# One step of a two-branch diffusion backbone in fp32 on one core: the residual kept in DRAM between the two halves of the output projection, and lanes and loaded weights in the lasting pool

## The chip, the cores and the metric

The kernel runs on 1 core of one Trainium2 chip. The metric is the device time of one execution in microseconds (us); the time of a kernel is the median of several runs. One execution is also recorded by the hardware profiler, and all rows below are from that one.

## The reference, cut to what matters

640 tokens (512 latent, 128 context) of width 2048 go through one layer. Everything is fp32. The modulation vectors come from a product of the conditioning vectors with a weight of 2048 x 12288.

```python
mod_ctx = silu(c_ctx) @ w_ada + b_ada        # the same for the latent tokens with c
shift1, scale1, gate1, shift2, scale2, gate2 = split(mod, 6)
h = rms_norm(x, g_norm1) * (1 + scale1) + shift1
proj = h @ w_in                              # query, compressed kv, rotary key, and three conv streams
attn = attention(...)                        # 8 heads, 1024 columns
conv = short_conv(...)                       # 1024 columns
mixed = concat([rms_norm(attn, g_attn_out), rms_norm(conv, g_conv_out)]) @ w_out
x = x + gate1 * mixed
h2 = rms_norm(x, g_norm2) * (1 + scale2) + shift2
gate, up = split(h2 @ w_gate_up, 2)          # 2 x 5632 columns
x = x + gate2 * ((silu(gate) * up) @ w_down)
y = rms_norm(x, g_final)
```

## The kernel before

All matrices lie transposed, features on the 128 partitions and the 640 tokens in two halves of 320, so a tensor of width 2048 is 16 tiles `R` of 128x640. Each fp32 product is made of three: both sides are split into a high and a low part (`split`: ScalarE casts the high part, L139, VectorE subtracts it, L140; `split_mul`, L144/L145, does so with a factor), and TensorE multiplies high by high, high by low and low by high (`mm3`, L162). A weight block of 512 KB is loaded by the SP queue into a `wr` tile and split by `wsplit` into `wh` and `wl`.

The stages follow each other, and one scheduler with a timeline model sets the order of the instructions on each engine ahead of time; the tile pools add the waits for free buffers.

- The modulation's first third (`ada1`) and eight early columns of the input projection.
- 31 more input projections (`proj`), 24 of them for the convolution branch, then attention over 8 heads.
- The output projection in two parts of 16 half projections each (one 512 KB weight and 48 matmuls of width 320 for each). Part 1 takes the convolution heads `nv`; it makes the gated residual `x1[m]` with `add_gated` (one VectorE multiplication, L606, and two VectorE additions with a scalar, L608). Beside it `na`, the attention heads with their gain, are split (L139, L145). Part 2 takes `na`, adds to `x1[m]` in place, sums its squares (`add_sq`: ScalarE square, L223, GpSimd addition, L224, VectorE for the last two), multiplies by the second scale into `u` (L670), stores `x1[m]` to DRAM (L673), and for each pair of m makes the seven-product operands `hs` (`splits`: sums on L636 to L639, casts and splits by L139 and L140).
- `r2 = rstd(ssq)`, the second rms factor: a matmul with ones (L205), logarithm and exponential on ScalarE (L207, L211), four VectorE steps (L208, L212 to L214).
- The first half of the feed-forward: 44 mids, and in each four units of 42 matmuls (`seven`, L715: seven products p1 to p3, each of two k-steps and three part products). `weights` loads 512 KB, sums three blocks (L697 to L699) and splits the loaded part (128x768) and the summed part (128x1024) on L139 and L140. VectorE then combines the seven PSUM banks (L735 to L741), GpSimd multiplies gate and up by `r2` (L742, L743), and ScalarE and VectorE make silu times up (L745, L746). `keep` and `sums` write the split results to DRAM (`parts`).
- The second half (`w_down`, also by `seven`), which loads `parts` by GpSimd's queue (L774), then a short tail.

The rest of the modulation (`ada2`) is work in the background: 8 blocks of 16 steps; a step loads 512 KB into `aw` and makes two VectorE operations of 128x1024 on `acc` (L260, L262), and a block ends with matmuls, a copy and additions (L269 to L279). `background(2)` is called with each weight split and gives out `RATES` steps for each of the two; `rest_of_background` gives out all that are left.

Memory: the pool `sb` lasts the whole program and holds 57 tiles `R`. The lanes `T1`, `T2` and `acc`, `aw`, `wr`, `wh`, `wl` are in a pool `first` that is closed at the end of the output projection; a pool `second` with `T1`, `T2`, `wr`, `ws`, `wh`, `wl` takes its place. In part 2 the 57 tiles hold `na` (16), `x1` (16), `ra`, `ssq`, and 7 for each pair of `hs`, so that from the fifth pair on `hs` waits for tiles of `na`, which the last half projection of part 2 reads.

## Time and profile before

| what | us |
|---|---|
| median of 3 runs | 2748.19 |
| lowest and highest | 2748.03, 2751.26 |
| the profiled execution | 2750.71 |
| its span | 2748.9 |
| TensorE busy in it | 2671.1 (97%) |
| VectorE busy in it | 2214.3 (81%) |

PE is TensorE's matmul stream, DVE is VectorE, ACT ScalarE, POOL GpSimd, SP the queue that loads weights. A row of the timeline gives the start, the duration, the instruction, and in brackets how long its engine stood idle before it and what released it. Rows of equal instructions are merged (x4) and their duration is that of all of them; since matmuls are pipelined, the distance of two starts tells more than a duration.

### The profile page before, as it was taken

To read this page: it belongs to the slowest core of one execution; us is meant where nothing else is said; L and a number is where in the kernel's file an instruction comes from. 1 tells how busy PE (TensorE), PEld (TensorE's weight loads), DVE (VectorE), ACT (ScalarE), POOL (GpSimd) and SP (SyncE) were. 2 spreads that over 40 slices of the span, in tenths; PEclk is the share of its full clock that TensorE was granted. 3 is DMA by queue.
4 is the path that set the end of the run, shared out by engine and by line. 5 is a ranking of instruction groups with operands and counts; after the bars stand their busy time and mean duration, and the time that the engine had idled before them with its cause. 6 is when DMAs were issued, how large, how long until landed. Compare 5 with 4: busy or idle time off the path is not lost.

```text
span 2748.9 us, 46698 instructions
## 1 busy us (share of the span) xinstructions
PE 2671.1 (97%) x18840; PEld 2625.9 (96%) x18840; DVE 2214.3 (81%) x3257; ACT 1024.5 (37%) x1550; POOL 402.5 (15%) x395
## 2 busy tenths in 40 slices
...
GB/s 306 288 191 187 185 192 175 189 182 62 16 151 178 187 161 83 120 123 147 118 131 139 118 152 118 123 147 119 131 139 128 272 230 156 290 161 178 214 186 143
DMA packets 156776, 447.85 MB, mean 163 GB/s; under 512 B 17104, under 2 KB 27792, under 8 KB 156560
## 3 DMA queue, kind: packets, MB, share of 16 engines
...
HBM read 366.66 MB, written 78.15 MB: 162 GB/s over the span
## 4 chain that ended last, share of the span: by engine, by line
PE 92%; DVE 4%; ACT 2%; issue 1%; DMA 1%; SPq 0%; ACTq 0%; DVEq 0%
PE bank L715 58%; PE psA L162 27%; PE bank L847 2%; PE psA L533 1%; PE psB L240 1%; DVE wl L140 1%; PE psB L562 1%; DVE acc L262 1%; DVE r L140 0%; PE psB L557 0%; ACT wh L139 0%; PE psB L269 0%; DMA t<-x 0%; DVE r L608 0%; ACT r L139 0%
## 5 line engine op out<-in xcount | busy, mean ns | idle before, releaser
L715 PE MATMUL bank<-r,wh 128*128 128x322 f32 (+1 forms) x7168 | 1594.5, 311 | 9.3 <-ACT wh L139 5.8
L715 PEld LDWEIGHTS bank<-r,wh 128*128 128x128 f32 x7168 | 1209.7, 189 | 10.6 <-ACT wh L139 6.8
L715 PE MATMUL bank<-r,wl 128*128 128x322 f32 (+1 forms) x3584 | 1112.8, 311 | 2.3 <-DVE wl L140 2.3
L139 ACT CAST wh<-wr 128x768 fp32r<-128x768 f32 (+1 forms) x370 | 333.0, 901 | 1121.6 <-issue 504.9
L162 PE MATMUL psA<-r,wh 128*128 128x322 f32 (+1 forms) x3584 | 693.5, 315 | 25.8 <-ACT r L139 11.0
L715 PEld LDWEIGHTS bank<-r,wl 128*128 128x128 f32 x3584 | 678.5, 189 | 2.7 <-DVE wl L140 2.7
L140 DVE TENSOR_TENSOR wl<-wr,wh 128x768 fp32r<-128x768 f32 (+1 forms) x370 | 422.9, 1143 | 246.1 <-ACT wh L139 245.8
L162 PEld LDWEIGHTS psA<-r,wh 128*128 128x128 f32 x3584 | 569.6, 190 | 41.5 <-ACT r L139 12.1
L162 PE MATMUL psA<-r,wl 128*128 128x322 f32 (+1 forms) x1792 | 415.9, 314 | 0.4 <-DVE wl L140 0.4
L140 DVE TENSOR_TENSOR wl<-ws,wh 128x1024 fp32r<-128x1024 f32 x256 | 366.0, 1430 | 31.2 <-ACT wh L139 31.1
L262 DVE SCALAR_TENSOR_TENSOR acc<-aw,sc,acc 128x1024 f32<-128x1024 f32 x240 | 302.6, 1299 | 7.9 <-DMA aw<-ada 7.8
L162 PEld LDWEIGHTS psA<-r,wl 128*128 128x128 f32 x1792 | 303.6, 190 | 3.4 <-issue 2.6
L139 ACT CAST wh<-ws 128x1024 fp32r<-128x1024 f32 x256 | 268.4, 1048 | 90.3 <-DVE ws L699 90.3
L743 POOL TENSOR_TENSOR t<-t,r 128x640 f32<-128x640 f32 x44 | 68.8, 1564 | 914.9 <-DVE t L740 914.9
L224 POOL TENSOR_TENSOR r<-r,t 128x640 f32<-128x640 f32 x42 | 79.0, 1880 | 811.7 <-ACT t L223 766.0
L697 DVE TENSOR_TENSOR ws<-wr 128x512 f32<-128x512 f32 x256 | 177.4, 693 | 5.5
L698 DVE TENSOR_TENSOR ws<-ws,wr 128x256 f32<-128x256 f32 x256 | 108.0, 422 | 5.6
L699 DVE TENSOR_TENSOR ws<-ws,wr 128x256 f32<-128x256 f32 x256 | 108.8, 425 | 4.4
L774 POOL DMA_DIRECT2D r<-parts x140 | 77.2, 564 | 159.5 <-PE bank L715 105.4
L355 DVE TENSOR_TENSOR r<-psA,r 128x644 f32<-128x644 f32 x64 | 52.4, 824 | 53.6 <-PE psA L162 53.6
L742 POOL TENSOR_TENSOR t<-t,r 128x640 f32<-128x640 f32 x44 | 93.6, 2127 | 0.8 <-DVE t L741 0.8
L745 ACT ACTIVATE t<-t 128x512 f32<-128x512 f32 x88 | 44.8, 557 | 111.8 <-POOL t L742 111.8
(180 smaller groups left out, 1907.3 us busy)
## 6 DMA issues: line engine op xcount, KB each, us to landing
...
aw<-ada SPq DMA_DIRECT2D x128, 512.0 KB, 4.3
parts<-t ACTq DMA_DIRECT2D x140, 320.0 KB, 4.2
r<-parts POOLq DMA_DIRECT2D x140, 320.0 KB, 6.7
...
```

The costliest lines, as they stand in the source:

```text
L139: A.copy(hi, src)
L140: return V.tensor_tensor(lo, src, hi.bitcast(F32), op=ALU.subtract)
L162: newest[T] = T.matmul(out[:, j, 0:n], w[p], x[q][:, j, 0:n], start=first and i == 0, stop=last and i == 2).ins
L224: e.tensor_tensor(acc, acc, qv, op=ALU.add)
L262: V.scalar_tensor_tensor(acc[v], w, sc[:, k, v:v + 1], acc[v], op0=ALU.mult, op1=ALU.add)
L697: V.tensor_tensor(q[:, :, 0:2], b[:, :, 1:4:2], b[:, :, 0:1].broadcast_to([P, 2, 2, P]), op=ALU.add)
L698: V.tensor_tensor(q[:, :, 2], q[:, :, 1], b[:, :, 1], op=ALU.add)
L699: V.tensor_tensor(q[:, :, 3], q[:, :, 2], b[:, :, 2], op=ALU.add)
L715: newest[T] = T.matmul(ps[name][:, 0:n], w[p][:, kp, i, :], xs[kp][x][q][:, 0:n], start=u + kp + t == 0, stop=u == len(units) - 1 and kp + ...
L742: G.tensor_tensor(row(g), row(g), r2, op=ALU.mult)
L743: G.tensor_tensor(row(up), row(up), r2, op=ALU.mult)
L774: nc.gpsimd.dma_start(t, two(parts[i][:, k], 320))
```

## The change

- In part 1, `add_gated` stores each `x1[m]` to DRAM from ScalarE's queue; in part 2 the SP queue loads it two half projections ahead into a fresh `R` tile and `add_gated` stores the sum again (before, it stayed in its tile and was stored once). So the 16 tiles of `x1` no longer stay.
- The last two `na` tiles lie in the buffers of `acc` and `aw` instead of `R`, and `u` of m = 10 to 13 lies in `R`.
- `T1`, `T2` and `wr` move from `first` and `second` to the lasting pool; `second` has one tile `hl` for high and low parts in the place of `wh` and `wl`.
- The rates of the modulation sums: 0.92 in the convolution projections (0.85), 1.1 in the query projections, 0 in attention, 0.83 in part 1 (0.85); what is left comes after m = 13 of part 1, and none in part 2 (0.6).
- `rstd` for the second factor is called between the second and the third unit of the first mid. Its matmuls go to two separate banks, and it writes into `ssq`.
- In the last two mids VectorE in place of GpSimd multiplies by the factor.

The diff:

```diff
--- before.py
+++ after.py
@@ -40,7 +40,9 @@
 
-FIRST = dict(T1=4, T2=3, acc=2, aw=2, wr=3, wh=3, wl=3)
-SECOND = dict(T1=4, T2=3, wr=3, ws=1, wh=3, wl=3)
+
+LASTS = dict(T1=4, T2=3, wr=3)
+FIRST = dict(acc=2, aw=2, wh=3, wl=3)
+SECOND = dict(ws=1, hl=3)
 NEARLY = 8
 GROUPS = [(0,), (1,)] + [(k, k + 1) for k in range(2, KT, 2)]
-RATES = (0.85, 0.0, 0.85, 0.6)
+RATES = (0.92, 1.1, 0.83)
 
@@ -50,2 +52,3 @@
             ("p4", 2, "t4", 322), ("p5", 4, "n1", 320), ("p3", 6, "b22", 320))
+LASTING = (10, 11, 12, 13)
 LAG = 1
@@ -86,6 +89,6 @@
     def T1(dtype=F32, shape=(P, 2, 320), name="t1"):
-        return bpool.tile(list(shape), dtype, name=name, tag="T1", bufs=bufs["T1"])
+        return pool.tile(list(shape), dtype, name=name, tag="T1", bufs=LASTS["T1"])
 
     def T2(dtype=F32, shape=(P, 2, 320), name="t2"):
-        return bpool.tile(list(shape), dtype, name=name, tag="T2", bufs=bufs["T2"])
+        return pool.tile(list(shape), dtype, name=name, tag="T2", bufs=LASTS["T2"])
 
@@ -95,3 +98,4 @@
     def tagged(tag, shape, n=None, dtype=F32):
-        return bpool.tile(list(shape), dtype, name=tag, tag=tag, bufs=n or bufs[tag])
+        p = pool if tag in LASTS else bpool
+        return p.tile(list(shape), dtype, name=tag, tag=tag, bufs=n or LASTS.get(tag) or bufs[tag])
 
@@ -197,3 +201,3 @@
 
-    def rstd(ssq, width, halves=(0, 1), out=None, wide=False):
+    def rstd(ssq, width, halves=(0, 1), out=None):
 
@@ -201,9 +205,7 @@
         v, t = T2(), T1()
-        pa = psA() if wide else None
-        ps = {j: pa[:, j, 0:320] if wide else psB()[:, 0:320] for j in halves}
-        for j in halves:
-            T.matmul(ps[j], ones, ssq[:, j, :], start=True, stop=True)
         for j in halves:
-            A.activation(t[:, j, :], ps[j], AF.Ln, bias=eps, scale=1.0 / width)
-            V.tensor_scalar(v[:, j, :], ps[j], 1.0 / width, EPS, op0=ALU.mult, op1=ALU.add)
+            ps = psB()[:, 0:320]
+            T.matmul(ps, ones, ssq[:, j, :], start=True, stop=True)
+            A.activation(t[:, j, :], ps, AF.Ln, bias=eps, scale=1.0 / width)
+            V.tensor_scalar(v[:, j, :], ps, 1.0 / width, EPS, op0=ALU.mult, op1=ALU.add)
         hs = slice(halves[0], halves[-1] + 1)
@@ -450,2 +452,3 @@
         add_sq(cssq, t, c == 0)
+    credit[1] = RATES[1]
     for h in range(1, NH):
@@ -573,4 +576,4 @@
 
-    def gain(t, g):
-        hl = R(F32R), R(F32R)
+    def gain(t, g, brief=False):
+        hl = [tagged(tag, (P, 2, 320), dtype=F32R) if brief else R(F32R) for tag in ("acc", "aw")]
         split_mul(*hl, t, g)
@@ -578,3 +581,3 @@
 
-    credit[1] = RATES[1]
+    credit[1] = 0.0
     kv = kv_pair(0)
@@ -603,3 +606,3 @@
 
-    def add_gated(ps, r, m):
+    def add_gated(x, ps, r, m):
         t = T1()
@@ -607,5 +610,6 @@
         for v, f in PARTS:
-            V.scalar_tensor_tensor(f(x1[m]), f(t), mod2[:, m, v:v + 1], f(x1[m]), op0=ALU.mult, op1=ALU.add)
+            V.scalar_tensor_tensor(f(x), f(t), mod2[:, m, v:v + 1], f(x), op0=ALU.mult, op1=ALU.add)
+        nc.scalar.dma_start(two(x1d[m], 320), x)
 
-    x1 = []
+    x1d = [dr(f"x1_{m}", (P, 640)) for m in range(KT)]
     credit[1] = RATES[2]
@@ -619,9 +623,11 @@
         for m in range(KT):
-            ps = proj(a["w_out"][m], nv, (0,))
-            x1.append(R())
-            nc.sync.dma_start(x1[m], a["x"][m])
-            add_gated(ps, rc, m)
+            x = R()
+            nc.sync.dma_start(x, a["x"][m])
+            add_gated(x, proj(a["w_out"][m], nv, (0,)), rc, m)
+            if m == 13:
+                rest_of_background()
+                credit[1] = 0.0
             if m >= 8:
                 with after(last_of(A), last_of(V)):
-                    na.append(gain(attn.pop(0), cst("gattn")[:, m - 8:m - 7]))
+                    na.append(gain(attn.pop(0), cst("gattn")[:, m - 8:m - 7], m > 13))
             if m == 12:
@@ -661,14 +667,17 @@
     hs, us = [], []
-    x1d = [dr(f"x1_{m}", (P, 640)) for m in range(KT)]
-    credit[1] = RATES[3]
+    x1 = {}
     for m in range(KT):
-        add_gated(proj(a["w_out"][m], na, (1,)), ra, m)
-        add_sq(ssq, x1[m], m == 0, G if m < KT - 2 else V)
+        for i in range(m, min(m + 2, KT)):
+            if i not in x1:
+                x1[i] = R()
+                nc.sync.dma_start(x1[i], two(x1d[i], 320))
+        x = x1[m]
+        add_gated(x, proj(a["w_out"][m], na, (1,)), ra, m)
+        add_sq(ssq, x, m == 0, G if m < KT - 2 else V)
 
-        u = (T1 if m % 2 else T2)(F32, (P, 2, 322))
+        u = (R if m in LASTING else T1 if m % 2 else T2)(F32, (P, 2, 322))
         for v, f in PARTS:
-            A.mul(f(u), f(x1[m]), mod2[:, 32 + m, v:v + 1])
+            A.mul(f(u), f(x), mod2[:, 32 + m, v:v + 1])
         G.tensor_copy(u[:, 0, 320:322], mod2[:, 16 + m, :])
         G.memset(u[:, 1, 320:322], 0.0)
-        nc.scalar.dma_start(two(x1d[m], 320), x1[m])
         us.append(u)
@@ -677,9 +686,7 @@
             us = []
-    del na, x1
+    del na, x1, x
 
 
-    r2 = rstd(ssq, D, wide=True)
     psums.close()
     psum = psums.enter_context(tc.tile_pool(name="ps8", bufs=1, space=bass.MemoryType.PSUM, reuse_waits="tile"))
-    rest_of_background()
     brief_pools.close()
@@ -694,3 +701,4 @@
         nc.sync.dma_start(b, src)
-        hi, lo = tagged("wh", (P, 2, 7, P), dtype=F32R), tagged("wl", (P, 2, 7, P), dtype=F32R)
+        hl = tagged("hl", (P, 2, 2, 7, P), dtype=F32R)
+        hi, lo = hl[:, 0], hl[:, 1]
         split(hi[:, :, 0:3], lo[:, :, 0:3], b[:, :, 1:4])
@@ -703,3 +711,3 @@
 
-    def seven(units):
+    def seven(units, between=None):
 
@@ -707,2 +715,5 @@
         for u, (src, xs) in enumerate(units):
+            if u == 2 and between:
+                with after(newest[T]):
+                    between()
             w = weights(src)
@@ -730,3 +741,5 @@
     for i in range(NMID):
-        ps = seven([(a["w_gu"][i, u], hs[2 * u:2 * u + 2]) for u in range(NU)])
+        ps = seven([(a["w_gu"][i, u], hs[2 * u:2 * u + 2]) for u in range(NU)],
+                   None if i else lambda: rstd(ssq, D, out=ssq))
+        r2 = ssq
         e, g, up = T1(F32, (P, 2, 322)), T1(F32, (P, 2, 322)), T2(F32, (P, 2, 322))
@@ -741,4 +754,5 @@
         V.tensor_tensor(g[:, 1, 0:320], ps["p3"][:, 0:320], u4, op=ALU.add)
-        G.tensor_tensor(row(g), row(g), r2, op=ALU.mult)
-        G.tensor_tensor(row(up), row(up), r2, op=ALU.mult)
+        by = G if i < NMID - 2 else V
+        by.tensor_tensor(row(g), row(g), r2, op=ALU.mult)
+        by.tensor_tensor(row(up), row(up), r2, op=ALU.mult)
         for v, f in PARTS:
@@ -758,3 +772,3 @@
                 keep((d[:, 2 * k + 1], d[:, 2 * k + 2]), T1(F32R), row(t))
-    del hs, r2, b1
+    del hs, r2, ssq, b1
```

How the order of the instructions moves is shown at three places. Line numbers of after differ from those of before: L264 is L262 before, L609 is L606, L611 is L608, L144 is L140, L149 is L145, L281 is L279, L226 is L224, L643 is L637, L705 to L707 are L697 to L699, L726 is L715.

VectorE where part 1 ends and part 2 begins, before (t_9630 and t_9702 belong to part 2's m = 0 and 1):

```order
L145 SCALAR_TENSOR_TENSOR r<-r,const 128x640
L262 SCALAR_TENSOR_TENSOR acc<-aw,sc,acc 128x1024 x4
L606 TENSOR_TENSOR t_9630<-psA,r 128x640
L140 TENSOR_TENSOR wl<-wr,wh 128x1024
L262 SCALAR_TENSOR_TENSOR acc<-aw,sc,acc 128x1024 x2
L608 SCALAR_TENSOR_TENSOR r<-t_9630,mod_80,r 128x2x256
L608 SCALAR_TENSOR_TENSOR r<-t_9630,mod_80,r 128x2x64
L606 TENSOR_TENSOR t_9702<-psA,r 128x640
L140 TENSOR_TENSOR wl<-wr,wh 128x1024
L262 SCALAR_TENSOR_TENSOR acc<-aw,sc,acc 128x1024 x2
```

The same place after (t_9606 and t_9672 belong to part 1's m = 14 and 15, t_9741 and t_9809 to part 2's m = 0 and 1; `aw<-r,const,acc` are the last two of `na`):

```order
L609 TENSOR_TENSOR t_9672<-psA,r 128x640
L144 TENSOR_TENSOR wl<-wr,wh 128x1024
L264 SCALAR_TENSOR_TENSOR acc<-aw,sc,acc 128x1024 x4
L281 TENSOR_TENSOR mod_80<-psB,const 128x16
L149 SCALAR_TENSOR_TENSOR r<-r,const 128x640
L611 SCALAR_TENSOR_TENSOR r<-t_9606,mod_80,r 128x2x256
L611 SCALAR_TENSOR_TENSOR r<-t_9606,mod_80,r 128x2x64
L611 SCALAR_TENSOR_TENSOR r<-t_9672,mod_80,r 128x2x256
L611 SCALAR_TENSOR_TENSOR r<-t_9672,mod_80,r 128x2x64
L149 SCALAR_TENSOR_TENSOR aw<-r,const,acc 128x640 x2
L609 TENSOR_TENSOR t_9741<-psA,r 128x640
L609 TENSOR_TENSOR t_9809<-psA,r 128x640
```

The last four modulation sums now stand ahead of part 2, then comes one of the gains into `R`, the additions of m = 14 and 15 and the two gains into `aw`, in a row; behind them the sums are gone. On TensorE the sixty matmuls of m = 0 and 1 that use the first five heads now stand ahead of the sixteen ones matmuls (L271) and four transposes (L278) of the last block of sums, on which L281 waits, and the matmuls with the last three heads stand behind those.

VectorE from the last half projection of part 2 to the first unit of the feed-forward, before (t_10900 is the last sum of `hs`):

```order
L140 TENSOR_TENSOR r<-t_10899,r 128x644
L140 TENSOR_TENSOR r<-t_10900,r 128x644
L208 TENSOR_SCALAR t_10921<-psA 128x320 x2
L212 TENSOR_TENSOR t_10922<-r 128x640
L213 SCALAR_TENSOR_TENSOR t_10922<-t_10922,t_10921 128x640
L214 SCALAR_TENSOR_TENSOR r<-t_10922,r 128x640
L697 TENSOR_TENSOR ws<-wr 128x2x256
L698 TENSOR_TENSOR ws<-ws,wr 128x2x128
L140 TENSOR_TENSOR wl<-wr,wh 128x2x384
L699 TENSOR_TENSOR ws<-ws,wr 128x2x128
L140 TENSOR_TENSOR wl<-wr,wh 128x2x384
```

The same place after (t_10866 and t_10934 are the products of part 2's m = 14 and 15):

```order
L705 TENSOR_TENSOR ws<-wr 128x2x256
L144 TENSOR_TENSOR r<-t_10788,r 128x644
L611 SCALAR_TENSOR_TENSOR r<-t_10866,mod_80,r 128x2x256
L611 SCALAR_TENSOR_TENSOR r<-t_10866,mod_80,r 128x2x64
L144 TENSOR_TENSOR hl<-wr,hl 128x2x384 x3
L706 TENSOR_TENSOR ws<-ws,wr 128x2x128
L144 TENSOR_TENSOR r<-t_10789,r 128x644
L611 SCALAR_TENSOR_TENSOR r<-t_10934,mod_80,r 128x2x256
L611 SCALAR_TENSOR_TENSOR r<-t_10934,mod_80,r 128x2x64
L226 TENSOR_TENSOR r<-r,t_10871 128x640
L144 TENSOR_TENSOR r<-t_10874,r 128x322
L707 TENSOR_TENSOR ws<-ws,wr 128x2x128
```

The rows of `rstd` are gone from here (they stand some twenty rows later, in the first mid), and the first units' splits (`hl<-wr`) stand among the last steps of part 2 instead of behind them.

TensorE around the end of mid 19 of the first half, before (p5 and p3 are the products of width 320; a unit is 30 matmuls of width 322 and 12 of width 320):

```order
L715 MATMUL bank<-r,wh 128x320 x2
L715 MATMUL bank<-r,wl 128x320
L715 MATMUL bank<-r,wh 128x320 x2
L715 MATMUL bank<-r,wl 128x320
L715 MATMUL bank<-r,wh 128x322 x2
L715 MATMUL bank<-r,wl 128x322
L715 MATMUL bank<-r,wh 128x322 x2
L715 MATMUL bank<-r,wl 128x322
L715 MATMUL bank<-r,wh 128x322 x2
L715 MATMUL bank<-r,wl 128x322
```

The same place after (`hl` holds the high and the low part, so neighbouring rows of one width are printed as one):

```order
L726 MATMUL bank<-r,hl 128x322 x9
L726 MATMUL bank<-r,hl 128x320 x8
L726 MATMUL bank<-r,hl 128x322 x17
L726 MATMUL bank<-r,hl 128x320 x4
L726 MATMUL bank<-r,hl 128x322 x8
L726 MATMUL bank<-r,hl 128x320 x8
L726 MATMUL bank<-r,hl 128x322 x32
L726 MATMUL bank<-r,hl 128x320 x12
L726 MATMUL bank<-r,hl 128x322 x24
L726 MATMUL bank<-r,hl 128x320 x4
```

Before, a unit's 42 matmuls stand product by product, and the next unit behind them; after, the last products of a unit are cut in two pieces (x4 and x8 of width 320), and the first products of the next unit stand between and ahead of them. This pattern runs through all mids.

## Rows read from the trace of the kernel before

**Rows 1.** The page, chain that ended last: share of each engine.
```profile
PE 92%; DVE 4%; ACT 2%; issue 1%; DMA 1%; SPq 0%; ACTq 0%; DVEq 0%
```

**Rows 2.** Busy time by stretch: length, PE, PEld, DVE, ACT, POOL, clock, DMA share, GB/s.
```profile
183.00:648.40 465.40, 465.14 (x3233) 462.82 (x3234) 384.03 (x438) 112.99 (x150) 12.57 (x7) 1.00 0.56 178
815.60:931.60 116.00, 115.67 (x828) 113.91 (x829) 97.39 (x117) 29.64 (x35) 2.03 (x4) 1.00 0.55 173
931.60:1061.40 129.80, 118.74 (x806) 117.41 (x804) 122.57 (x150) 55.94 (x86) 37.63 (x38) 0.96 0.46 148
1061.40:1081.00 19.60, 6.25 (x17) 4.55 (x18) 15.28 (x26) 12.90 (x18) 1.03 (x4) 0.58 0.09 27
1081.00:2197.60 1116.60, 1116.60 (x7507) 1116.29 (x7506) 974.56 (x1462) 439.11 (x578) 180.75 (x126) 1.00 0.43 139
2197.60:2205.00 7.40, 3.92 (x16) 3.92 (x17) 7.33 (x16) 3.79 (x6) 3.78 (x7) 0.77 1.06 305
```

**Rows 3.** Timeline of PE in part 2: start, us, instruction, idle before.
```profile
931.67 0.74 PE L162 MATMUL psA<-r,wh 128*128 128x320 f32 x4
...
975.58 0.83 PE L162 MATMUL psA<-r,wh 128*128 128x320 f32 x4 [1.54 <-ACT r L139]
...
995.19 1.40 PE L162 MATMUL psA<-r,wh 128*128 128x320 f32 x4 [5.30 <-ACT r L139]
...
1029.76 0.84 PE L162 MATMUL psA<-r,wh 128*128 128x320 f32 x4 [4.15 <-ACT r L139]
```

**Rows 4.** Timeline of DVE ahead of the wait at 995.
```profile
982.43 2.47 DVE L262 SCALAR_TENSOR_TENSOR acc<-aw,sc,acc 128x1024 f32<-128x1024 f32 x2
...
988.61 3.76 DVE L262 SCALAR_TENSOR_TENSOR acc<-aw,sc,acc 128x1024 f32<-128x1024 f32 x2
...
994.24 1.54 DVE L606 TENSOR_TENSOR t<-psA,r 128x640 f32<-128x640 f32 x2
```

**Rows 5.** Groups of DVE by form, 929 to 1062: count, busy us, mean ns.
```profile
L262 DVE SCALAR_TENSOR_TENSOR acc<-aw,sc,acc 128x1024 f32<-128x1024 f32 x30 | 42.2, 1448 | 0.0
```

**Rows 6.** Timeline of PE from the end of part 2 to the first mid.
```profile
1060.73 0.60 PE L276 MATMUL psB<-const,ev 128*128 128x128 f32 x4
1066.57 2.47 PE L205 MATMUL psA<-r,ones 128*128 128x320 f32 x4 [5.24 <-DVE r L224]
1074.88 1.44 PE L715 MATMUL bank<-r,wh 128*128 128x322 f32 x4 [5.84 <-ACT wh L139]
1078.66 0.64 PE L715 MATMUL bank<-r,wl 128*128 128x322 f32 x1 [2.35 <-DVE wl L140]
...
1080.98 1.06 PE L715 MATMUL bank<-r,wh 128*128 128x322 f32 x4
```

**Rows 7.** Timeline of ACT and of DVE in that stretch.
```profile
1078.98 1.05 ACT L139 CAST wh<-ws 128x1024 fp32r<-128x1024 f32 x1 [3.41 <-DVE ws L699]
...
1078.86 0.95 DVE L140 TENSOR_TENSOR wl<-wr,wh 128x768 fp32r<-128x768 f32 x1
1080.06 1.23 DVE L140 TENSOR_TENSOR wl<-ws,wh 128x1024 fp32r<-128x1024 f32 x1 [0.24 <-ACT wh L139]
```

**Rows 8.** Timeline where `w_down` begins: POOL, DVE, PE.
```profile
2190.06 1.45 POOL L743 TENSOR_TENSOR t<-t,r 128x640 f32<-128x640 f32 x1
...
2196.05 0.96 DVE L140 TENSOR_TENSOR wl<-wr,wh 128x768 fp32r<-128x768 f32 x1 [6.19 <-ACT wh L139]
...
2201.08 0.81 PE L715 MATMUL bank<-r,wh 128*128 128x320 f32 x2 [3.49 <-DVE t L787]
```

**Rows 9.** Groups by form, 1081 to 2195: POOL, and two of DVE.
```profile
L742 POOL TENSOR_TENSOR t<-t,r 128x640 f32<-128x640 f32 x44 | 93.6, 2127 | 0.8 <-DVE t L741 0.8
L140 DVE TENSOR_TENSOR wl<-ws,wh 128x1024 fp32r<-128x1024 f32 x180 | 272.9, 1516 | 29.7 <-ACT wh L139 29.7
L726 DVE TENSOR_TENSOR t<-t,t 128x640 fp32r<-128x640 f32 x63 | 49.8, 815 | 0.0
```

**Rows 10.** The page, DMA issues: KB each, median us to landing.
```profile
r<-x SPq DMA_DIRECT2D x32, 320.0 KB, 6.6
```

## The prediction

> **What bounds the kernel now.** The chain that ended last comes first: TensorE holds 92% of it, DVE 4% [rows 1]. So a gain can come only from stretches in which TensorE stands still or runs slowly, and the question is where these are. The busy time by stretch tells it [rows 2]. In the convolution projections PE is busy in 465.1 of 465.4 us while DVE has 81 us free; in part 1 of the output projection PE is busy throughout and DVE in 97.4 of 116.0. In part 2, with the same 768 matmuls, 129.8 us pass at a mean granted clock of 0.96, and DVE is busy in 122.6 of them. Between part 2 and the first mid 19.6 us pass at clock 0.58. The first half of the feed-forward, 1116.6 us, is full on PE, and DVE is busy for 87% of it. Where `w_down` begins there is one more hole of some microseconds. These three places (part 2, the boundary behind it, the begin of `w_down`) are all that the change can win; all else it can only spoil.
>
> Part 2 is bound by DVE. PE stops for 1.54, 5.30 and 4.15 us [rows 3]. The profile puts this down to a cast on ACT, but the second stop ends at 995.19, just when DVE's first product of L606 (from 994.24, 0.8 us) has emptied a PSUM tile, and ahead of that DVE worked off modulation sums, two of them in 2.47 us and two in a stretch of 3.76 [rows 4]. Thirty such sums stand in part 2, 42.2 us by the profile, 37 if a pair costs 2.47 [rows 4, 5].
>
> **Part 2.** The stops add up to 11.0 us. Behind the second one four matmuls take 1.40 us, against 0.83 behind the shortest [rows 3]: the engine had stood still for 5.3 us and then ran at the lower of its levels (1.2 against 2.4 GHz), which is where the clock of 0.96 comes from [rows 2]. By the difference to part 1, 129.7 less 116.0, the loss is 13.7; with 3 to 4 us for slow stretches it is 14 to 15. I take 14.5. After, the sums are gone from part 2, DVE has some 85 us of work in 115, and the stops in its middle have no cause left. In their place comes one at its start, by the order of after. DVE's L281 waits for the transposes, which on PE stand behind sixty matmuls with the first five heads (60 x 0.147 = 8.8 us). After it come the gain for the sixth head, four additions for m = 14 and 15, and two more gains, at 0.8 us for an operation of that size [rows 9] and about 1 for a pair of additions 4.6 us in all. PE has only the twelve matmuls of the sixth head, 1.8 us, to lay beside that, and a PSUM copy and two hand-overs, 1.5 us, come on top: a stop of 4.4. Gain 10; ends 0 (the new stop as long as the old ones) and 14 (none).
>
> **The sums elsewhere.** Twenty-two more sums go into the convolution and query projections, 27 us into 81 free ones [rows 2, 4]; PE's cover there is its own full queue, and I cost them at nothing. Four more go into part 1, and DVE comes to some 107 of 116 us there. If this leaves DVE late inside part 1, it costs up to 2 us. I take 1.
>
> **The residual through DRAM.** Sixteen more stores on ACT's queue and sixteen loads on SP's. What is queued behind a load on SP is the next weight; the load itself only waits for the store of two projections' age and for a free tile. A projection takes 7.2 us (116.0 / 16), and a load of this size, issued in a batch, 6.6 [rows 10], so that two projections ahead it is hidden. This holds for all but m = 13 to 15, whose tiles are those of three `na`, and these are read for the last time in the last projection. They are loaded about 8 us before its end; so at worst m = 14 and 15 are a microsecond or two late, at the boundary. Nothing for the first thirteen, 0 to 3 for the rest, which the boundary below includes.
>
> The Trainium skill, DMA: Bandwidth & Descriptors, Anatomy of one DMA, gives a transfer on the software path some 2.0 us fixed and bytes / 436e3, 2.75 us for 320 KB, and this speaks against a way through DRAM in general, since the store and the load each pay the fixed part. The rows agree that a transfer has a price far above its bytes, and show a larger one; by the page's figure the last loads would come about 4 us earlier and the sum would not move.
>
> **The boundary.** Before: the last matmul of a projection ends at 1060.7, and from 1080.98 on PE runs without a hole [rows 6]. In between lie 14 matmuls of the first mid, 2.1 us at 0.149, so the start is worth 1078.9 and the loss 18.2. On the way PE waits 5.24 us for the last squares, 5.84 for a cast behind the factor's ScalarE steps, 2.35 for a split [rows 6]. After, the factor is computed inside the first mid, and PE no longer stands behind it; its two matmuls still cost 1.2. The `hs` of the first six pairs are ready early, and only the last two wait for `na`. But `hl` lies over `wh`, `wl`, `acc` and `aw` of the last projection, so that ScalarE's first cast cannot begin before PE's end. From there: cast 0.8, split 0.95 [rows 7], and p1 and p2 of three units, 36 matmuls, 5.4 us, have their operands after 4 us. The next that PE wants is the summed part of the first unit, and its split stands on DVE behind three splits of 0.95, two sums, the additions for the last m, two square sums and the last `hs` sums: with 0.8 for each large one [rows 9] and half of that for each half one about 13 us, and with waits for ACT's squares and casts, which I estimate at 2.4, about 15.4 after the end. Of these 5.4 are filled: a loss of 10. Gain 18.2 - 10 - 1.2 = 7; ends 3 (late loads of m = 14, 15) and 11 (DVE without waits).
>
> **The first half of the feed-forward.** The work of a mid is the same, but the order of PE is not. Units now lie one in another in a pattern of two mids, and summed parts are wanted as soon as they are made. Adding durations along the order (ACT cast 1.05, DVE splits 0.95 and 1.23; DVE is busy 44.3 us of the 50.8 of a pair of mids [rows 2, 7]), I find every operand in time, the tightest, a cast of a summed part in the third unit, by 0.9 us. So nothing; the price of being wrong is in the first rival, since it would be paid 22 times. In the first mid DVE has a backlog from the boundary: 0 to 1, I take 0.5.
>
> DVE's split of 128x1024 takes 1.23 us at the boundary, where POOL is idle, and 1.516 on average in the mids [rows 7, 9]. The Trainium skill, SBUF — State Buffer, two separate sides, says that a DVE operation with two SBUF inputs and a GpSimd operation exclude each other on a shared pair of ports; the rows agree in sign. By that rule the splits under POOL's `r2` product would come 0.3 to 1 us later than I added above and the slack of 0.9 would be about gone, which would make the first rival likelier but not price it.
>
> **The begin of `w_down`.** Before, GpSimd's product for the last mid starts at 2190.06 only, in a queue of loads, silu waits for it, DVE idles 6.19 us behind a cast that waits in turn, and PE stops 3.49 us and then runs slow for four us [rows 8]: 5.0 lost. With the last two mids' products on DVE (four of 0.82 [rows 9]: 3.3 us into at least 6 idle ones) the chain doesn't touch POOL's queue. Gain 4.5; ends 0 and 5.
>
> **Sum.** 10 - 1 + 7 - 0.5 + 4.5 = 20. The profiled execution took 2750.7 (1.8 above its span), so it would take 2730.7; it was 2.5 above the median of 2748.2, and the forecast stands against the median: 2728.
>
> **Rivals.** *Just in time fails (slower).* If the interleaved units make PE wait once in each pair of mids, the price is 22 times the wait. For: DVE is at 87%, the slack is 0.9 us, and POOL makes single DVE splits longer [rows 2, 9]. Against: the order is fixed, so a delay of PE gives DVE the same time back. At 0.5 us the time is 2739; at 0.9 the gain is gone; from 1.2 (26 us) on the kernel is slower; at 1.6 it is 2763.
>
> *The wait moves to the start of part 2.* If DVE is behind at the end of part 1 (107 of 116 us, last sums in a burst), the new stop takes all of the 10: 2738.
>
> *The boundary stays as long.* `hl` waits for PE's end, and the last loads for `na`: if both come in sequence with the squares, as 5.24 us of waiting for them before [rows 6], the 7 us are gone: 2735. For it: all of DVE's last work still lies there. Against: the factor's two ScalarE steps and three DVE steps no longer do.
>
> *The change does not do what it says:* both of these, and the begin of `w_down` is held up by something else than POOL: 2747 to 2750, no change.
>
> **Chances.** The forecast 0.55; wait at the start of part 2 0.13; boundary 0.12; just in time fails mildly (2733 to 2742) 0.08; fails badly (slower) 0.06; no change 0.06. The measurement tells apart about 0.2%, 5.5 us. Faster is the first four: 0.88; within 0.2% 0.06; slower 0.06. The forecast's own range goes from 2717 (all upper ends: 14 + 11 + 5 = 30) to 2733; with the milder rivals the range is 2717 to 2742.
>
> **What would show it.** In the profile after: no modulation sum in part 2, DVE busy for some 85 us there, PE with one stop of 3 to 6 us in its first two projections and none later; `rstd`'s ones matmuls between matmuls of the first mid, and a hole of 8 to 12 us at the boundary, ended by a split of 128x1024; PE full from there to `w_down`; no stop over 1 us at its begin. Wrong would be: stops of PE that repeat every 50 us in the mids, a clock below 1.00 there, a stop above 10 us at the start of part 2, or a convolution stage over 466 us.

## The result and the profile after

The changed kernel takes 2725.97 us (median of 4 runs, 2725.77 to 2726.32) against 2748.26 us (4 runs); the ratio is 0.9917 with an interval of 0.9899 to 0.9934. The forecast was 2728, with a range of 2717 to 2742. The profiled execution took 2726.06 us, its span is 2724.3, 24.6 less than that of before.

Busy time by stretch, after; the columns are those of [rows 2]:

```profile
183.00:648.40 465.40, 465.40 (x3259) 461.92 (x3258) 409.02 (x460) 113.56 (x151) 12.87 (x7) 1.00 0.60 190
815.60:931.60 116.00, 114.73 (x796) 113.22 (x796) 100.71 (x114) 29.30 (x34) 1.95 (x3) 1.00 0.65 207
931.60:1061.40 129.80, 121.13 (x833) 118.87 (x832) 97.93 (x140) 62.39 (x96) 25.99 (x43) 0.97 0.47 153
1061.40:1081.00 19.60, 18.63 (x122) 17.93 (x121) 15.68 (x26) 9.96 (x14) 0.00 (x0) 1.00 0.31 98
1200.00:1500.00 300.00, 300.00 (x2028) 300.00 (x2026) 265.38 (x398) 117.58 (x156) 45.30 (x24) 1.00 0.40 132
2180.00:2205.00 25.00, 25.00 (x173) 25.00 (x172) 21.09 (x35) 12.05 (x18) 10.69 (x18) 1.00 1.14 372
```

DVE's work has gone from the third stretch (122.6 before, 97.9 now) into the first (384 before, 409 now). The stretch from 1061 to 1081, almost empty before, is full, and PE no longer stops near 2200. The hole between part 2 and the mids is still there; it lies earlier now, in the third stretch, and that is why its clock is still 0.97.

The executions differ by some microseconds ahead of part 1 (its first mark stands at 815.6 in before and at 811.5 in a kernel below that is changed far behind it only), so that two traces can't be laid on each other by time. Each stage is measured between marks of its own: the same wait in the first projection of part 1, the last matmul of part 2, and the first matmul of the tail. The first and the last mark, before and then after, in the timeline of PE:

```profile
815.60 0.56 PE L162 MATMUL psA<-r,wh 128*128 128x320 f32 x2 [0.75 <-DVE r L145]
...
2677.50 12.78 PE L847 MATMUL bank<-r 128*128 128x384 f32 x72
```

```profile
818.10 0.56 PE L166 MATMUL psA<-r,wh 128*128 128x320 f32 x2 [0.76 <-DVE r L149]
...
2652.29 38.05 PE L861 MATMUL bank<-r 128*128 128x384 f32 x228
```

The last matmul of part 2 ends at 1060.9 before and 1049.9 after. So parts 1 and 2 (from the first mark) took 245.3 us and take 231.8; from there to the tail 1616.6 and 1602.4. The stages ahead of the first mark are 2.5 us longer, the tail is 0.6 longer: -13.5 - 14.2 + 2.5 + 0.6 = -24.6. Of the 14.2, by the count of matmuls done, 4.9 lie in the first three mids with the boundary ahead of them, 4.0 in the other 41 mids, and 5.3 behind the mids, where `w_down` begins.

**The start of part 2**, after, on PE:

```profile
941.24 1.08 PE L271 MATMUL psB<-acc,ones 128*32 128x128 f32 x32
943.03 0.66 PE L278 MATMUL psB<-const,ev 128*128 128x128 f32 x4 [0.71 <-ACT ev L274]
...
946.90 0.84 PE L166 MATMUL psA<-acc,wh 128*128 128x320 f32 x4 [0.72 <-ACT acc L148]
...
951.35 0.85 PE L166 MATMUL psA<-r,wh 128*128 128x320 f32 x4 [0.33 <-DVE t L609]
```

and on DVE:

```profile
934.65 4.96 DVE L264 SCALAR_TENSOR_TENSOR acc<-aw,sc,acc 128x1024 f32<-128x1024 f32 x4
943.72 0.17 DVE L281 TENSOR_TENSOR mod<-psB,const 128x16 f32<-128x16 f32 x1 [4.11 <-PE psB L278]
...
946.88 1.81 DVE L149 SCALAR_TENSOR_TENSOR aw<-r,const,acc 128x640 fp32r<-128x640 f32 x2 [0.34 <-ACT acc L148]
```

DVE waits at L281 for the transposes, as the order said, and the chain behind it takes 5 us. But PE stops for 0.71, 0.72 and 0.33 only, and then for nothing until the end of part 2. The long stops of [rows 3] are gone.

**The boundary**, after, on PE, ACT, DVE and POOL:

```profile
1049.45 0.46 PE L166 MATMUL psA<-acc,wl 128*128 128x320 f32 x2
1052.81 0.86 PE L726 MATMUL bank<-r,hl 128*128 128x322 f32 x4 [2.90 <-ACT hl L143]
1057.40 12.78 PE L726 MATMUL bank<-r,hl 128*128 128x322 f32 x74 [3.73 <-DVE hl L144]
1071.15 6.54 PE L726 MATMUL bank<-r,hl 128*128 128x322 f32 x42 [0.97 <-ACT hl L143]
1077.53 0.70 PE L208 MATMUL bank<-r,ones 128*128 128x320 f32 x2
...
1051.29 0.73 ACT L143 CAST r<-t 128x644 fp32r<-128x644 f32 x1 [1.04 <-DVE t L642]
1051.92 2.30 ACT L143 CAST hl<-wr 128x768 fp32r<-128x768 f32 x3
...
1049.55 1.65 DVE L642 TENSOR_TENSOR t<-r 128x322 f32<-128x322 f32 x1 [0.51 <-ACT r L680]
...
1056.40 2.68 DVE L144 TENSOR_TENSOR hl<-wr,hl 128x768 fp32r<-128x768 f32 x3
...
1064.43 1.21 DVE L144 TENSOR_TENSOR hl<-ws,hl 128x1024 fp32r<-128x1024 f32 x1
...
1049.30 1.55 POOL L226 TENSOR_TENSOR r<-r,t 128x640 f32<-128x640 f32 x1 [4.38 <-ACT t L225]
```

and the granted clock there, by stretches of 2 us, columns as above with PE alone:

```profile
1054.00:1056.00 2.00, 0.00 (x0) 0.50 0.00 0
1056.00:1058.00 2.00, 0.60 (x2) 0.50 0.33 131
1058.00:1060.00 2.00, 2.00 (x10) 0.50 0.09 33
1060.00:1062.00 2.00, 2.00 (x14) 0.91 0.02 9
```

PE waits 2.90 us for the first cast and 3.73 for the first split, and because it stood, its clock falls to the lower level (1.2 GHz, 0.50 here) and comes back only after 1060. The ones matmuls of the factor stand inside the first mid and wait for nothing. The first cast begins at 1051.92, 2.0 us after PE's last work: on ACT a cast for the last `hs` stands ahead of it, and that one waits for a sum of DVE that took 1.65 us beside an addition of GpSimd (the same sum takes 0.48 at 1063.62).

**The begin of `w_down`**, after: the product by `r2` is on DVE, and PE has one unbroken row where it stopped for 3.49 us in [rows 8].

```profile
2164.78 20.43 PE L726 MATMUL bank<-r,hl 128*128 128x320 f32 x138
```

### The profile page after: what moved, and what is told of

The parts are those of the page before. It is cut to its first block, busy times and chain, and to the rows that moved or that the text cites. A ratio compares the mean times of both kernels' runs of the same rounds, so it can differ in the third digit from the quotient of the medians.

```text
span 2724.3 us, 46612 instructions
## 1 busy us (share of the span) xinstructions
PE 2663.4 (98%) x18840; PEld 2617.4 (96%) x18840; DVE 2211.6 (81%) x3261; ACT 1023.6 (38%) x1550; POOL 386.8 (14%) x391
## 4 chain that ended last, share of the span: by engine, by line
PE 60%; DVE 1%; ACT 0%; issue 0%; DMA 0%; ACTq 0%; DVEq 0%
PE bank L726 58%; PE bank L861 2%; DVE hl L144 0%; ACT hl L143 0%; DVE t L849 0%; DMA o_y<-t 0%; DVE ws L705 0%; PE bank L843 0%; DVE t L737 0%; DVE r L144 0%; PE bank L835 0%; PE bank L208 0%; DVE t L760 0%; DVE r L611 0%; DVE t L645 0%
## 5 line engine op out<-in xcount | busy, mean ns | idle before, releaser
L726 PE MATMUL bank<-r,hl 128*128 128x322 f32 (+1 forms) x10752 | 1592.6, 310 | 9.7 <-ACT hl L143 4.9
L726 PEld LDWEIGHTS bank<-r,hl 128*128 128x128 f32 x10752 | 1589.5, 189 | 12.4 <-ACT hl L143 6.9
L166 PE MATMUL psA<-r,wh 128*128 128x322 f32 (+1 forms) x3456 | 667.5, 314 | 15.6 <-ACT wh L143 6.3
L143 ACT CAST hl<-ws 128x1024 fp32r<-128x1024 f32 x256 | 268.6, 1049 | 498.6 <-DVE ws L707 495.6
L144 DVE TENSOR_TENSOR hl<-ws,hl 128x1024 fp32r<-128x1024 f32 x256 | 315.7, 1233 | 120.5 <-ACT hl L143 120.5
L144 DVE TENSOR_TENSOR hl<-wr,hl 128x768 fp32r<-128x768 f32 x256 | 263.0, 1028 | 93.7 <-ACT hl L143 93.6
L143 ACT CAST hl<-wr 128x768 fp32r<-128x768 f32 x256 | 212.9, 833 | 271.6 <-issue 190.6
L264 DVE SCALAR_TENSOR_TENSOR acc<-aw,sc,acc 128x1024 f32<-128x1024 f32 x240 | 298.9, 1281 | 15.5 <-DMA aw<-ada 14.7
L143 ACT CAST wh<-wr 128x1024 fp32r<-128x1024 f32 x114 | 119.2, 1050 | 379.2 <-PE psA L166 310.9
L705 DVE TENSOR_TENSOR ws<-wr 128x512 f32<-128x512 f32 x256 | 223.4, 873 | 3.9
L226 POOL TENSOR_TENSOR r<-r,t 128x640 f32<-128x640 f32 x42 | 75.0, 1785 | 832.1 <-ACT t L225 831.6
L144 DVE TENSOR_TENSOR wl<-wr,wh 128x1024 fp32r<-128x1024 f32 x114 | 142.7, 1251 | 7.3 <-ACT wh L143 7.2
L707 DVE TENSOR_TENSOR ws<-ws,wr 128x256 f32<-128x256 f32 x256 | 129.7, 507 | 5.6
```

The lines of the kernel that those rows point to most:

```text
L143: A.copy(hi, src)
L144: return V.tensor_tensor(lo, src, hi.bitcast(F32), op=ALU.subtract)
L166: newest[T] = T.matmul(out[:, j, 0:n], w[p], x[q][:, j, 0:n], start=first and i == 0, stop=last and i == 2).ins
L226: e.tensor_tensor(acc, acc, qv, op=ALU.add)
L264: V.scalar_tensor_tensor(acc[v], w, sc[:, k, v:v + 1], acc[v], op0=ALU.mult, op1=ALU.add)
L705: V.tensor_tensor(q[:, :, 0:2], b[:, :, 1:4:2], b[:, :, 0:1].broadcast_to([P, 2, 2, P]), op=ALU.add)
```

## The experiments

The theory was that three places give the gain, each for a reason of its own: the sums in part 2, the chain at the boundary, and GpSimd's queue where `w_down` begins. Rival A: in part 2 it was memory, held by `x1`, and not the sums. Rival B: at `w_down` it was the new order of the matmuls, and not GpSimd. Rivals C and D come with their runs. Medians are of kernels compared with before on one chip, but not all on the same one: before took 2750.4 us beside b_rates, b_byv, a_byg and a_sums_e, 2749.9 beside a_rstd_first, a_pools, a_x1_kept and v3_hs_late, and 2749.7 beside the last four (after_again, x1_kept_hs_late, b_rates_byv and a_whwl). Stage lengths are from the profile of each, between the marks above. The last three columns divide the stretch from the end of part 2 to the tail by the count of matmuls done (168 to a mid), since in some kernels the units lie one in another. The diffs show the lines that matter; `...` stands for what is left out.

| kernel | us | ratio to before, interval | parts 1 and 2 | end of part 2 to tail | first 3 mids | other 41 mids | behind the mids |
|---|---|---|---|---|---|---|---|
| before | 2748.3 |  | 245.3 | 1616.6 | 93.6 | 1024.5 | 498.6 |
| after | 2726.0 | 0.9917 (0.9899 to 0.9934) | 231.8 | 1602.4 | 88.7 | 1020.4 | 493.3 |
| after_again | 2726.2 | 0.9914 (0.9899 to 0.9929) | 231.8 | 1602.7 | 88.7 | 1020.8 | 493.3 |
| b_rates | 2740.5 | 0.9967 (0.9954 to 0.9980) | 235.4 | 1613.2 | 93.1 | 1021.7 | 498.4 |
| b_byv | 2745.7 | 0.9981 (0.9971 to 0.9990) | 245.3 | 1611.2 | 93.6 | 1024.5 | 493.2 |
| b_rates_byv | 2736.1 | 0.9948 (0.9932 to 0.9965) | 235.4 | 1608.4 | 93.4 | 1021.7 | 493.4 |
| a_byg | 2737.4 | 0.9957 (0.9942 to 0.9972) | 231.8 | 1613.1 | 88.2 | 1020.7 | 504.3 |
| a_sums_e | 2748.7 | 0.9993 (0.9984 to 1.0003) | 252.7 | 1608.2 | 90.0 | 1024.2 | 494.0 |
| a_rstd_first | 2731.6 | 0.9933 (0.9918 to 0.9948) | 231.8 | 1608.6 | 91.7 | 1023.6 | 493.3 |
| a_pools | 2734.7 | 0.9944 (0.9929 to 0.9959) | 231.8 | 1610.9 | 93.6 | 1024.5 | 492.8 |
| a_x1_kept | 2728.1 | 0.9919 (0.9903 to 0.9936) | 234.1 | 1600.2 | 84.6 | 1022.2 | 493.4 |
| a_whwl | 2727.4 | 0.9917 (0.9902 to 0.9932) | 231.8 | 1603.4 | 88.3 | 1021.8 | 493.3 |
| v3_hs_late | 2725.0 | 0.9909 (0.9894 to 0.9924) | 231.8 | 1602.0 | 87.3 | 1021.0 | 493.7 |
| x1_kept_hs_late | 2727.7 | 0.9919 (0.9904 to 0.9934) | 235.4 | 1600.5 | 84.0 | 1023.2 | 493.4 |

### The sums alone (b_rates)

```diff
-RATES = (0.85, 0.0, 0.85, 0.6)
+RATES = (0.92, 1.1, 0.83)
+    credit[1] = RATES[1]
...
-    credit[1] = RATES[1]
+    credit[1] = 0.0
...
+            if m == 13:
+                rest_of_background()
+                credit[1] = 0.0
...
-    credit[1] = RATES[3]
...
-    rest_of_background()
```

> The kernel before with one part of the change alone: the modulation sums at the new rates, the rest of them after m = 13 of part 1, none in part 2. x1, the tiles and the second factor stay as before. Theory of the forecast (the sums bind VectorE in part 2): the three stops in the middle of part 2 vanish, one of 1 to 4 us comes at its start, part 2 is 10 to 12 us shorter and nothing else moves: 2736 to 2739 us. Rival A (part 2 stood still because the hs and u tiles waited for memory that the x1 tiles held): the stops stay and the time is 2745 or more.

Measured: 2740.5, 9.9 us below before. PE's waits in it, from part 2 to the first mid:

```profile
942.42 0.42 PE L269 MATMUL psB<-acc,ones 128*32 128x128 f32 x8 [1.39 <-DVE acc L262]
943.61 1.33 PE L269 MATMUL psB<-acc,ones 128*32 128x128 f32 x24 [0.77 <-DVE acc L262]
945.63 1.11 PE L276 MATMUL psB<-const,ev 128*128 128x128 f32 x4 [0.69 <-ACT ev L272]
...
1058.53 2.47 PE L205 MATMUL psA<-r,ones 128*128 128x320 f32 x4 [5.32 <-DVE r L224]
1068.71 1.44 PE L717 MATMUL bank<-r,wh 128*128 128x322 f32 x4 [7.71 <-ACT wh L139]
```

and the granted clock behind the stops at the start of part 2, with PE alone:

```profile
946.00:948.00 2.00, 2.00 (x9) 0.50 0.00 0
```

The stops in the middle of part 2 are gone with the sums alone, with `x1` in its old tiles. At its start three are left, 2.9 us in all, and behind them PE runs at the lower level until 950; in after it stops for less there and the clock stays at 1.00. Rival A falls. The boundary is as it was: PE waits for the last squares and then for a cast behind the factor. The time is 1.5 us above the 2736 to 2739 that were expected. Parts 1 and 2 are 9.9 shorter, near what was expected; but something else moves too: the stages ahead of part 1 are 3.5 longer, as in after, and the 41 mids 2.7 shorter.

### The sums back in part 2 (a_sums_e)

```diff
-RATES = (0.92, 1.1, 0.83)
+RATES = (0.85, 0.0, 0.85, 0.6)
...
-            if m == 13:
-                rest_of_background()
-                credit[1] = 0.0
...
-                    na.append(gain(attn.pop(0), cst("gattn")[:, m - 8:m - 7], m > 13))
+                    na.append(gain(attn.pop(0), cst("gattn")[:, m - 8:m - 7]))
...
+    credit[1] = RATES[3]
...
+    rest_of_background()
```

> The changed kernel with the old rates, so that 26 modulation sums lie in part 2 again; the last two na tiles lie in R, since acc and aw are then in use. Theory: VectorE is full in part 2 again, stops of 8 to 13 us in all come back there, 2734 to 2740 us. Rival A: with x1 in DRAM the tiles are free, part 2 stays as short as in the changed kernel, 2725 to 2728 us.

Measured: 2748.7; nearly all of the gain is lost, about twice what was expected. PE's longest waits:

```profile
986.16 1.41 PE L166 MATMUL psA<-r,wh 128*128 128x320 f32 x4 [11.26 <-ACT r L143]
...
1079.24 17.39 PE L724 MATMUL bank<-r,hl 128*128 128x322 f32 x98 [5.57 <-DVE mod L281]
```

Parts 1 and 2 take 252.7 us, more than before; the longest wait is again put down to a cast, and ends just when DVE, behind its sums, has emptied a PSUM tile (L608 from 985.20, 0.8 us). And the closing steps of the last sums now stand on PE's path at the boundary, where before they ran beside the factor's chain. So the other parts of the change are worth little without this one. What they gain behind the mids (494.0 us against 498.6) is still there; part 2 loses more than it had lost before, and why more was not taken apart.

### VectorE for the last two products, alone and undone (b_byv, a_byg)

```diff
-        G.tensor_tensor(row(g), row(g), r2, op=ALU.mult)
-        G.tensor_tensor(row(up), row(up), r2, op=ALU.mult)
+        by = G if i < NMID - 2 else V
+        by.tensor_tensor(row(g), row(g), r2, op=ALU.mult)
+        by.tensor_tensor(row(up), row(up), r2, op=ALU.mult)
```

This is b_byv's change to before; a_byg has `by = G` in the changed kernel.

> The kernel before with VectorE in place of GpSimd for the r2 product of the last two mids, and nothing else. Theory of the forecast (the product stood in GpSimd's queue between loads of parts): the stop of 3.49 us and the slow matmuls behind it at the begin of w_down go, 2743 to 2744 us. Rival B (the stop goes only where TensorE's matmuls of the units lie one in another, so that weights are split earlier): the stop stays, 2748 us.

> The changed kernel with GpSimd for the r2 product in all mids, as before. Theory: the stop at the begin of w_down comes back, 3.5 to 5 us, 2729.5 to 2731 us. Rival B: no stop, 2726 us.

Measured: alone it gives 4.8 us (2745.7), 5.4 in the stage by its marks. Undone in after it costs 11.2 (2737.4 against 2726.2; 11.0 behind the mids), twice or three times what was expected. Rival B falls, since the stop goes in b_byv too, without the new order. In a_byg it is longer than in before; whether by the new order of the matmuls or by another part of the change, no run tells. The place in a_byg, POOL, then DVE, then PE:

```profile
2172.84 1.88 POOL L757 TENSOR_TENSOR t<-t,r 128x640 f32<-128x640 f32 x1
...
2175.81 1.45 POOL L756 TENSOR_TENSOR t<-t,r 128x640 f32<-128x640 f32 x1
...
2173.45 1.82 DVE L705 TENSOR_TENSOR ws<-wr 128x512 f32<-128x512 f32 x1
2175.18 2.90 DVE L144 TENSOR_TENSOR hl<-wr,hl 128x768 fp32r<-128x768 f32 x1
...
2187.18 13.09 PE L726 MATMUL bank<-r,hl 128*128 128x320 f32 x76 [9.37 <-DVE t L798]
```

GpSimd comes to the product only at 2172.84, behind its loads, and while it multiplies, two DVE operations that take 0.69 and 0.95 us elsewhere take 1.82 and 2.90. Both delays go into the same chain to silu, and PE stands for 9.37 us. In before DVE had nothing to do while GpSimd multiplied (idle for 6.19 us in [rows 8]).

### The sums and the products together (b_rates_byv)

The two changes above in the kernel before.

> The kernel before with two parts of the change, the sums out of part 2 and VectorE for the last two r2 products, and nothing of the tiles, of DRAM or of the factor. Theory (separate places, so the gains add): 10 and 5 us below before, 2734 to 2737 us, and the boundary holds the rest of the change's gain. Rival (one frees what the other needs): they add up to clearly less than 13 or more than 17.

Measured: 2736.1, 13.7 below before: the two add up within 1 us (9.9 and 4.8), with the memory, the residual and the factor left as they were. What those three give is the difference to after_again beside it, 9.9 us: 3.5 in parts 1 and 2, 4.7 in the first three mids, 1.0 in the other mids, the rest ahead of part 1 and in the tail. Of the changes of place, those of the last two `na` tiles and of `u` were not undone by themselves.

### The factor ahead of the first mid (a_rstd_first)

```diff
+    rstd(ssq, D, out=ssq)
     for i in range(NMID):
-                   None if i else lambda: rstd(ssq, D, out=ssq))
+                   None)
```

> The changed kernel with the second rms factor computed ahead of the first mid again (its matmuls to two banks, as in the changed kernel). Theory (the factor's chain stood on TensorE's path at the boundary): TensorE waits for the last squares and then for a cast behind the factor's ScalarE steps, the boundary is 5 to 9 us longer, 2731 to 2735 us. Rival C (the boundary is set by VectorE's last sums and splits, the factor is hidden beside them): 2726 to 2728 us. In this kernel the order of the mids' matmuls is product by product again, as in the kernel before; where the interleaved order costs something in the mids, the first half would be shorter by it.

Measured: 2731.6, 5.5 us above after. PE waits at the ones matmul until the last squares are summed:

```profile
1063.79 2.50 PE L208 MATMUL bank<-r,ones 128*128 128x320 f32 x4 [13.78 <-DVE r L226]
```

Only 3.0 us of the 5.5 lie at the boundary (91.7 us to the end of the third mid against 88.7), where 5 to 9 were expected; 3.2 lie in the other 41 mids, which the expectation left out as a cost. So rival C falls, and the theory has the cause right and its price about twice too high; that the time fell into its range is in part luck. The mids of this kernel run product by product, and take 24.967 us each against 24.888: the interleaved order costs nothing there.

### T1, T2 and wr in the short-lived pools (a_pools)

```diff
-LASTS = dict(T1=4, T2=3, wr=3)
-FIRST = dict(acc=2, aw=2, wh=3, wl=3)
-SECOND = dict(ws=1, hl=3)
+LASTS = {}
+FIRST = dict(T1=4, T2=3, wr=3, acc=2, aw=2, wh=3, wl=3)
+SECOND = dict(T1=4, T2=3, wr=3, ws=1, hl=3)
```

and `T1` and `T2` take their tiles from the short-lived pool again.

> The changed kernel with T1, T2 and wr in the pools first and second, as before. Theory: the first weights of the mids can then be loaded only when the tiles of first are given up, so one load (3.6 us and more) comes into the boundary, which is 3 to 8 us longer: 2729 to 2734 us. Rival: the place of these tiles does not matter since ScalarE's first cast waits for hl in any case: 2725 to 2727 us.

Measured: 2734.7, 8.6 us above after, a little over the upper end of what was expected. PE waits 15.06 us for the first cast of the mids:

```profile
1063.92 15.17 PE L726 MATMUL bank<-r,hl 128*128 128x322 f32 x84 [15.06 <-ACT hl L143]
```

The first weights are loaded from 1047.25 on (from 1018.15 on in after), and the first of them are there at 1051.32, 2.5 us after PE's last work. The cast begins at 1063.04 only: in the order of this kernel it stands on ACT behind all the work for the last `hs`. So by the rows PE waits in the end not for the late load but for the order that came out with it. The first three mids take 5.0 us more than in after, the other 41, product by product here too, 4.0 more.

In the first three mids this and the factor together would give 8.0 us (5.0 and 3.0), more than the 4.7 that after has over b_rates_byv there: each holds back the same start, and either alone is enough to lose most of it.

### x1 kept in its tiles (a_x1_kept)

```diff
-            x = R()
+            x = x1[m] = R()
...
-        for i in range(m, min(m + 2, KT)):
-            if i not in x1:
-                x1[i] = R()
-                nc.sync.dma_start(x1[i], two(x1d[i], 320))
```

and no store of `x1` in part 1.

> The changed kernel with x1 kept in its 16 R tiles from part 1 to part 2: no store in part 1, no load in part 2; all else as in the changed kernel. Theory (the way through DRAM frees tiles for the last hs, which TensorE wants at the boundary): hs of pairs 5 to 8 wait for na again, the boundary is 3 to 9 us longer and part 2 stays as short as it is: 2729 to 2735 us. Rival D (the tiles did not matter once the sums were gone): 2725 to 2727 us, with the loads saved.

Measured: 2728.1. PE's waits in it:

```profile
944.76 0.43 PE L271 MATMUL psB<-acc,ones 128*32 128x128 f32 x8 [1.07 <-DVE acc L264]
948.02 1.11 PE L278 MATMUL psB<-const,ev 128*128 128x128 f32 x4 [1.20 <-ACT ev L274]
...
1055.50 0.86 PE L723 MATMUL bank<-r,hl 128*128 128x322 f32 x4 [0.92 <-DVE r L611]
1059.21 17.87 PE L723 MATMUL bank<-r,hl 128*128 128x322 f32 x104 [2.85 <-DVE hl L144]
```

The first three mids are not longer but 4.1 us shorter than in after: PE waits 0.92 us ahead of them and not 2.90. The other 41 mids are 1.8 us longer, and parts 1 and 2 are 2.3 longer, since the order that came out puts the closing of the sums earlier on PE, which then waits for them. From the first mark to the tail the two profiles take the same, 1834.3 us and 1834.2. So the theory falls: the way through DRAM, the part that the change is named after, buys nothing in sum, though it moves time from one stage to another. Rival D comes nearest, and its time was 1 us too low. Of the 2.8 us by which its profile is longer, 2.4 lie ahead of the first mark (820.5, 818.1 in after), which that change doesn't reach; a_whwl, changed behind part 2 alone, begins part 1 at 820.2.

### wh and wl as before (a_whwl)

```diff
-SECOND = dict(ws=1, hl=3)
+SECOND = dict(ws=1, wh=3, wl=3)
...
-        hl = tagged("hl", (P, 2, 2, 7, P), dtype=F32R)
-        hi, lo = hl[:, 0], hl[:, 1]
+        hi, lo = tagged("wh", (P, 2, 7, P), dtype=F32R), tagged("wl", (P, 2, 7, P), dtype=F32R)
```

> The changed kernel with wh and wl as separate tiles in the second pool, as before, in the place of hl. Theory: their size and number are the same and a unit's high and low parts come free almost together, so no change within 1.5 us of the changed kernel. Rival: with two tiles the first cast need not wait for all of what lies under both, and the boundary is 1 to 3 us shorter.

Measured: 2727.4 (2724.8 to 2729.2), not told apart from after; the stops at its boundary are 2.88 and 3.73 us, as in after, so the rival falls.

### The last hs later (v3_hs_late, x1_kept_hs_late)

```diff
-        if m % 2:
+        if m % 2 and m < 13:
             hs.append(splits(*us, 322))
...
-            if u == 2 and between:
-                with after(newest[T]):
-                    between()
+            if u in (between or {}):
+                with after(newest[{1: V, 2: T}[u]]):
+                    between[u]()
...
-                   None if i else lambda: rstd(ssq, D, out=ssq))
+                   None if i else {1: late_hs, 2: lambda: rstd(ssq, D, out=ssq)})
```

`late_hs` makes the `hs` of m = 12 to 15.

> The changed kernel with the operands hs of the last two pairs (m = 12 to 15) made only behind the splits of the first unit's weights; the units that use them are the last of the mid. Theory (what is left at the boundary is VectorE's order: the first unit's summed part stands behind the last hs sums): the first unit's summed split comes 4 to 6 us earlier, the boundary loses 3 to 5 us less, 2721 to 2723 us. Rival: the last units then wait for their hs, and as much is lost there: 2725 to 2728 us.

Measured: 2725.0, 0.9 below after; from the end of part 2 to the tail 0.4 to 0.7 (1.4 less in the first three mids, 1.0 more behind them). The timeline of PE, and the clock in one stretch:

```profile
1052.44 0.86 PE L728 MATMUL bank<-r,hl 128*128 128x322 f32 x4 [2.63 <-ACT hl L143]
1054.20 19.69 PE L728 MATMUL bank<-r,hl 128*128 128x322 f32 x109 [0.89 <-DVE hl L144]
...
1076.97 0.81 PE L208 MATMUL bank<-r,ones 128*128 128x320 f32 x2 [1.50 <-ACT t L753]
```

```profile
1056.00:1058.00 2.00, 2.00 (x9) 0.50 0.33 61
```

The stop of 3.73 us is down to 0.89, as meant, and most of the gain does not come: the matmuls run at the lower level until 1060, to the time at which the clock rose in after too, and the factor's second matmul now waits 1.50 us for ACT. The rival holds, though by another way than it said.

In x1_kept_hs_late the same was done with `x1` kept and the factor one unit later.

> The changed kernel with x1 kept in its R tiles, the hs of the last two pairs behind the first unit's splits, and the second factor between the third and fourth unit. Theory now: the way through DRAM buys no time, and of the boundary's rest a part goes when the first unit's splits come early and the factor's matmuls stand where their ScalarE steps have room: 1 to 4 us less than the changed kernel in the same comparison, 2722 to 2726. Rival: the loads' absence makes the last hs or the start of part 2 late, as the last gains are in R's place: not less than the changed kernel.

Measured: 2727.7, no gain. From the end of part 2 to the tail it takes 1600.5 us, but parts 1 and 2 take 235.4, since PE waits at their start for the closing of the sums; the rival holds. No kernel here beats the changed one by more than the runs differ.

### The changed kernel again (after_again)

> The changed kernel itself once more, beside the other three, so that a few us can be compared on one chip: 2725 to 2727 us. If the 2.1 us by which the kernel with x1 kept in its tiles took longer lie in the run and not in the kernel, this one also comes out at 2727 to 2728.

Measured: 2726.2 (2725.9 to 2727.2), so the time of after repeats. It ran on another chip than a_x1_kept, but before took the same on both within 0.2 us. The 2 us by which a_x1_kept is longer aren't shown to belong to what was changed: its profile has them ahead of part 1.

## Why the prediction was right, step by step

- **What bounds the kernel.** Right. All three places lost time, and the sums, not the cast that the profile names, made part 2 wait: b_rates shows it.
- **Part 2.** A gain of 10 and 1 of cost in part 1 were forecast; parts 1 and 2 are 13.5 shorter, of which 3.5 came back ahead of them, so 10.0. The sums alone give 9.9 of the 13.5 (b_rates), the other parts of the change the rest. Three terms were mis-sized and cancel in part. "I cost them at nothing", of the sums in the convolution stage, is the step that failed: from the first factor's ones matmul to the end of the last query projection it takes 479.6 us against 477.4, and attention, from there to the first mark, is 1.4 longer. I had costed VectorE's part only; a block of sums also ends in ones matmuls and transposes on TensorE, 1.08 and 0.66 us in the rows of after, and with 22 more sums one more block ends there. In the three kernels with the old rates the stage takes 475.8 to 477.4 us, in the eleven with the new ones 478.0 to 479.6, so it goes with the rates. So does the stretch of attention (167.2 to 167.8 against 168.5 to 169.7), which was not taken apart. Against that, the new stop at the start of part 2 is 1.8 us and not 4.4: I let PE wait for both parts of the last heads, but it begins with the high ones, which ScalarE makes first, and the low ones come in time. And the 1 us in part 1 was not lost: VectorE has 101.6 us of work there and not 107, and PE has no stop that before hasn't.
- **The residual through DRAM.** Costed at nothing, and in sum that is right: a_x1_kept takes 1834.3 us from the first mark to the tail, after 1834.2. It isn't nothing in each stage, and the picture is not mine: without it part 2 begins 2.3 us worse and the first three mids are 4.1 shorter. These differences come with the order of the instructions; no run ties them to the tiles or to the loads.
- **The boundary.** A loss of 18.2 going to 10, and 1.2 and 0.5 in the first mid, so 6.5. The stops of after add up to 9.3 us (2.90, 3.73, 0.97, and 0.81 and 0.89 in the second and third mid), the lower clock costs some 2 (12 matmuls at twice the time) and each of five stops hides some 0.16 at its modelled end (the record of a matmul lasts 0.31 us, and the next starts 0.15 after it); that is about 12, and the factor's two matmuls take 0.6 and not 1.2, so the gain is 5 to 6. By the count of matmuls it is 4.9, faster mids included. The size is a little high and the picture is not right: I saw PE wait for the summed split, 15.4 us after the end, with 36 matmuls as cover. That split does end there (1064.43 + 1.21, 15.7 after 1049.9), but 62 matmuls stand ahead of the first that needs it (p4 doesn't use the sums, and high parts go first), so nothing waits for it. PE waits for the first cast and the first split instead, which I had 4 us after the end. The cast begins 2.0 after it, for ScalarE's order and not for `hl`: in a_x1_kept it begins at once (1054.62, PE's work ends at 1054.58). The split begins 6.5 after it, behind work for the last `hs`.
- **The begin of `w_down`.** 4.5 forecast; 4.8 by b_byv, 5.3 by the marks, and no stop in after. That the same step is worth 11.2 in after was not foreseen. The Trainium skill, SBUF — State Buffer, two separate sides, says that a GpSimd operation that reads SBUF and a DVE operation with two SBUF inputs exclude each other; the rows of a_byg agree (0.95 us alone, 2.90 beside GpSimd).
- **The first half.** "So nothing": the rival that fails just in time didn't occur; PE is full from 1200 on and single stops of 0.81 and 0.89 stand in the second and third mid only. But behind these three a mid takes 24.888 us on average instead of 24.987, which is 4.0 us in 41 mids and no part of my sum. It is no single gap: two matmuls start 148.1 ns apart on average and not 148.7. It isn't the interleaved order alone: b_rates (product by product) has 24.920 and a_sums_e (interleaved) 24.981. It repeats where the mids are the same (24.897 in after_again, 24.894 in a_byg; 24.920 in b_rates_byv as in b_rates). What makes it is open.
- **The signs.** VectorE is busy for 84 us in part 2, no stop comes in its middle, the mids show none that repeats, and no stop is left at the begin of `w_down`, as said. Others came out otherwise. The start of part 2 has three short stops, 1.8 us in all, instead of one of 3 to 6, and the last four sums still run beside its first matmuls. No split of 128x1024 ends the hole at the boundary. And the convolution stage, 465.4 us in before, is 2.1 longer and so over the 466 that I had named as a sign of being wrong: this is the cost of the sums there.
- **Two slips.** A pair of mids is 49.97 us long and not 50.8 (the stretch of [rows 2] reaches into `w_down`), and 30 less than 2748 is 2718 and not 2717; nothing hangs on either.

So the sum of 20 came out at 22.3 by the medians, and at 23.6 beside after_again. The stages give 10.0 for 9, about 5 for 6.5, 5.3 for 4.5, and some 4 in the mids that weren't in it, less 0.6 in the tail: 23.6. That the total is within 2 to 4 us of the forecast is in part luck, since 3.5 us of cost ahead of part 1 and 4 of gain in the mids, neither of them foreseen, stand against each other.
